# Attention values of layer 1 and of the stick-breaking block: attention weights as the stationary side, against values as the stationary side with two heads on the halves of the array's columns

## The chip, the core and the metric

The program runs on one core of one Trainium2 chip. The metric is device microseconds of one execution, the median of several runs. The program is one launch: weights are streamed from HBM, everything else stays on the core. The engines are TensorE (PE, with PEld for its weight loads), VectorE (DVE), ScalarE (ACT), GpSimd (POOL) and SyncE (SP), which issues the DMAs.

## What is computed

Two mixing layers and a second block, on 256 positions of width 1024, in float32. Two places matter here. Layer 1 (`moba_attention`) has 16 heads of 64; with 256 positions there is one block, so it is causal attention, followed by a gate and an output projection:

```python
s_own = jnp.einsum('bhqd,bhkd->bhqk', qc, kown).astype(jnp.float32)
p = masked_softmax(jnp.concatenate([s_sel, s_own], axis=-1) * scale, mask).astype(v.dtype)
o + jnp.einsum('bhqk,bhkd->bhqd', p[..., nk:], vown)
...
o = moba_attention(q, k, v, cos, sin) * jax.nn.silu(z)
return jnp.einsum('bse,ed->bsd', o, w_out)
```

The second block has a stick-breaking attention with 8 heads of 64, whose output goes into a projection without a gate of its own ahead of it:

```python
attn = jnp.where(causal, jnp.exp(jax.nn.log_sigmoid(z) + rest), 0.0)
return jnp.einsum("bhqk,bhkd->bhqd", attn.astype(v.dtype), v)
...
y_a = o @ w_attn_out[l]
```

## The kernel before

Positions lie in two tiles of 128 (`tt` = 0, 1). Each projection (`Proj`, line 694) accumulates a 128x512 output in an accumulator bank (`acc`), with three float32r matmuls for each 128 rows of the contraction (`mm3`, line 658): high by high, high by low and low by high part. Both sides are therefore split into a high part (ACT copy) and a low part (DVE subtraction): the weights after their DMA (`split`, line 651), the activations after a turn to feature-major on TensorE (`to_lhs`, line 827; the lists `oT`, `ya`, `hT` hold the two parts). These projections are the bulk of TensorE's work, the rows `acc<-kr,kr` of the profile.

In the names of the profile `k` stands for the plain SBUF pools, `kr` for the pool of split float32r tiles, `m` for the four working PSUM banks, `acc` for the four accumulators and `tiny` for small vectors. All instructions carry line 562 (or 563 in the changed kernel), that of the recording helper. Each float32 matmul of 128x64 and the like is two records in the trace, a transpose by the identity is one.

**Layer 1.** It works in two halves `j` of 8 heads. A unit (`o_unit`, line 1483, through `sm_unit`, line 883) takes four heads of tile 0 or two heads of tile 1: scores and a mask into one bank, maximum on DVE, exponential on ACT with the sum into `den1`, then a turn (four transposes, one ACT copy into `pt`), then the values: for each head and key block one matmul with the 128x128 piece of `pt` as the stationary side and the head's 64 columns of `v` as the moving side. There are 12 units, with four such matmuls each. The output is position-major, [128, 8, 64] in one bank for each (`j`, `tt`). `o_done` (line 1495) multiplies it by the reciprocal of twice the sums on DVE. `gated` (line 1344) multiplies by the gate `zz` (the silu of projection `odd3j`) on DVE and sends the product through `to_lhs`: four transposes, an ACT copy for the high part and a DVE subtraction for the low part. `mid1` (line 1531) does so for the second half of the heads, in the middle of the output projection `oo`.

**Stick-breaking.** `st_unit` (line 1703) makes one head: scores into a bank `z`, two ACT passes, a scan and a product on DVE, three transposes, one ACT copy `at`, then three value matmuls with 128x128 pieces of `at` stationary and 64 columns of `v` moving. After each four heads two ACT copies scale the bank into position-major tiles, and at the end `st_done` (line 1741) turns these with eight transposes, two ACT copies and two DVE subtractions into `ya`. Beside it DVE runs the 124 steps of a depthwise convolution (`conv_step`, line 1603), which are put in with a low priority.

**The order.** The program is recorded first, as a list of operations with their dependences. A list scheduler (`Order.solve`, line 284) then sets the order in which each engine's queue receives them, and the slots of the pools, from a table of durations (`cost`, line 508); `best` (line 271) takes the best of several rules and rounds. `od.fused()` ties consecutive operations into one that nothing is put between. Each engine runs its own queue in order and waits on semaphores. The order of one operation can therefore move others around it.

## Time and profile before

| | us |
|---|---|
| median of 3 runs | 759.78 |
| the three runs | 757.1, 759.78, 760.51 |
| the profiled execution, its own time | 761.01 |
| its span in the trace | 759.3 |
| TensorE busy | 733.1 (97%) |
| VectorE busy | 573.7 (76%) |
| ScalarE busy | 404.1 (53%) |
| granted TensorE clock, mean | 0.997 |

TensorE's busy time is the union of its records, whose ends are modelled; they overlap, so the mean of one record is longer than the time that it adds. The time of a matmul is better read from the starts of consecutive rows. Layer 1 attention lies between about 229 and 332 us of the span, the stick-breaking attention between about 390 and 468 us.

### The profile page before, as it was taken

What the parts mean: (1) busy time and instruction counts of PE and PEld (TensorE: products, weight loads), DVE (VectorE), ACT (ScalarE), POOL (GpSimd) and SP (SyncE); (2) the same over time, 40 slices, a digit from 0 to 9 for tenths busy, and PEclk for the clock granted to TensorE, in tenths of its full rate; (3) what the DMA queues carried; (4) which work ended last, traced back from release to release, by engine and by line L of the source; (5) the groups of instructions that cost most, each with busy time, mean ns of one, the idle gap of its engine ahead of it and who ended that gap; (6) DMA issues with size and microseconds to landing.
All of it is one profiled execution on the core that took longest, in us unless ns stands there. A gap on an engine that the chain in (4) does not pass through costs nothing.

```text
span 759.3 us, 10452 instructions
## 1 busy us (share of the span) xinstructions
PE 733.1 (97%) x3712; PEld 596.4 (79%) x3712; DVE 573.7 (76%) x1057; ACT 404.1 (53%) x715; POOL 13.7 (2%) x40
## 2 busy tenths in 40 slices
PE   3999999997999999999999999999999999999998
PEld 1887788786787888878877778878887888888886
DVE  4899899957987564598899999997857555646531
ACT  5565878747454546446455564566445444435420
POOL 1000000000000000001000000000000000000000
PEclk9999999999999999999999999999999999999999
DMA  8998978734684533456532476654747555645101
GB/s 325 400 372 285 368 251 297 236 130 140 210 289 136 196 129 114 148 191 209 182 113 84 139 226 208 206 184 174 250 139 253 191 195 173 214 140 193 57 1 55
DMA packets 43572, 148.08 MB, mean 195 GB/s; under 512 B 6272, under 2 KB 7424, under 8 KB 43520
## 3 DMA queue, kind: packets, MB, share of 16 engines
q1 hardware_dynamic: 43520, 147.41, 56.6%
q8 instruction: 29, 0.48, 0.3%
q14 instruction: 23, 0.19, 0.1%
HBM read 146.34 MB, written 1.05 MB: 194 GB/s over the span
## 4 chain that ended last, share of the span: by engine, by line
PE 76%; DVE 10%; DMA 7%; ACT 5%; issue 1%; SPq 0%; ACTq 0%; DVEq 0%
PE acc L562 65%; PE m L562 11%; DMA k<-in_wst_dram 7%; DVE k L562 5%; DVE kr L562 4%; ACT k L562 3%; ACT kr L562 2%; DVE x L562 1%; SPq L562 0%; DVE tiny L562 0%; DVE ab L562 0%; DVE keepA L562 0%; ACTq L562 0%; DVEq L562 0%
## 5 line engine op out<-in xcount | busy, mean ns | idle before, releaser
L562 PE MATMUL acc<-kr,kr 128*128 128x512 f32 x2520 | 653.7, 407 | 4.0 <-ACT kr L562 3.9
L562 PEld LDWEIGHTS acc<-kr,kr 128*128 128x128 f32 x2520 | 469.0, 190 | 103.2 <-ACT k L562 2.8
L562 DVE TENSOR_TENSOR kr<-k,kr 128x1024 fp32r<-128x1024 f32 (+3 forms) x234 | 265.9, 1151 | 85.8 <-PE acc L562 68.0
L562 ACT ACTIVATE kr<-k 128x1024 fp32r<-128x1024 f32 (+3 forms) x234 | 230.6, 1005 | 147.0 <-PE acc L562 98.1
L562 PE MATMUL m<-identf,k 128*128 128x128 f32 x414 | 97.5, 279 | 5.8 <-DVE k L562 4.8
L562 PE MATMUL m<-k,k 128*128 128x64 f32 (+4 forms) x436 | 75.3, 304 | 11.6 <-DMA k<-in_wst_dram 10.6
L562 PEld LDWEIGHTS m<-k,k 128*128 128x128 f32 (+1 forms) x436 | 67.1, 188 | 22.2 <-issue 12.2
L562 ACT ACTIVATE k<-m 128x512 f32<-128x512 f32 (+6 forms) x115 | 53.3, 471 | 39.7 <-PE m L562 38.3
L562 PEld LDWEIGHTS m<-identf,k 128*128 128x128 f32 x414 | 56.7, 146 | 20.8 <-DVE k L562 6.0
L562 DVE CUSTOM_DVE_ANT_0 k<-k,cb 128x1024 f32<-128x1024 f32 x44 | 53.0, 1216 | 2.4 <-DMA k<-in_wst_dram 2.3
L562 DVE SCALAR_TENSOR_TENSOR k<-k,col,k 128x256 f32<-128x256 f32 x128 | 54.2, 475 | 0.0
L562 ACT ACTIVATE k<-m,tiny 128x128 f32<-128x128 f32 (+1 forms) x80 | 32.9, 423 | 21.6 <-DVE tiny L562 18.9
L562 ACT ACTIVATE kr<-m 128x512 fp32r<-128x512 f32 (+3 forms) x52 | 24.9, 491 | 27.6 <-PE m L562 23.7
L562 DVE TENSOR_TENSOR kr<-m,kr 128x256 fp32r<-128x256 f32 (+2 forms) x44 | 23.8, 552 | 13.0 <-PE acc L562 7.5
L562 DVE TENSOR_REDUCE tiny<-m 128x2 f32<-128x512 f32 (+1 forms) x30 | 20.6, 687 | 7.8 <-PE m L562 7.5
L562 DVE TENSOR_TENSOR k<-k,k 128x512 f32<-128x512 f32 (+5 forms) x42 | 24.5, 591 | 0.3
L562 ACT ACTIVATE k<-acc,rf 128x256 f32<-128x256 f32 x22 | 10.3, 472 | 27.0 <-PE acc L562 26.8
L562 DVE SCALAR_TENSOR_TENSOR k<-acc,rf,k 128x256 f32<-128x256 f32 x22 | 10.5, 482 | 18.7 <-ACT k L562 18.5
L562 ACT ACTIVATE k<-k 128x512 f32<-128x512 f32 (+4 forms) x28 | 14.9, 538 | 13.6 <-DVE k L562 13.5
L562 PE MATMUL m<-kr,kr 128*128 128x408 f32 (+1 forms) x96 | 21.7, 329 | 0.1
L562 DVE TENSOR_TENSOR k<-acc,x 128x512 f32<-128x512 f32 x4 | 2.8, 691 | 22.4 <-PE acc L562 22.4
L562 ACT ACTIVATE k<-m,ab 128x128 f32<-128x128 f32 (+1 forms) x24 | 10.6, 489 | 14.9 <-DVE ab L562 14.9
(111 smaller groups left out, 319.9 us busy)
## 6 DMA issues: line engine op xcount, KB each, us to landing
k<-in_wst_dram SPq DMA_DIRECT2D x266, 512.0 KB, 4.5
k<-in_wst_dram SPq DMA_DIRECT2D x8, 204.0 KB, 8.1
k<-in_rows_dram SPq DMA_DIRECT2D x3, 512.0 KB, 3.5
k<-in_rows_dram SPq DMA_DIRECT2D x6, 256.0 KB, 5.5
x<-in_x_dram SPq DMA_DIRECT2D x2, 512.0 KB, 3.8
out_dram<-k SPq DMA_DIRECT2D x4, 256.0 KB, 2.0
cb<-in_rows_dram SPq DMA_DIRECT2D x1, 512.0 KB, 7.0
k<-in_w_dram SPq DMA_DIRECT2D x2, 128.0 KB, 5.9
```

The lines of the kernel that those rows point to most:

```text
L562: self._o.add(self._n, lambda: f(*a, **kw), method, writes, reads, info)
```

## The change

In layer 1 the roles of the value matmul are swapped: the 64 columns of `v` of one head are the stationary side, in one half of the array's columns, and the 128 columns of `pt` move. Two heads lie on the two halves (output partitions 0 to 63 and 64 to 127), and the four matmuls of a unit are tied together with `od.fused()`. Heads are now taken in sequence. The output is feature-major, [128, 4, 128]. The factor from the sums, which belongs to a position, can no longer be put on the output by a broadcast along its rows; it is put on the gate, position-major, and the gate is turned instead (`z_turn`): one DVE product, four transposes, one ACT copy. `o_done` copies the output out of PSUM with ACT; `gated_t` multiplies on DVE and splits into high and low part from SBUF.

In the stick-breaking block the values are swapped in the same way for a pair of heads at a time: two matmuls of 256 and two of 128 moving columns. The output is already feature-major, so the high and low parts are taken straight from PSUM, with the factor 0.5, and the two position-major tiles, the four scaling copies and `st_done` with its eight transposes are gone. The table of durations gets an entry for outputs of 64 partitions.

```diff
-            return (d / 4 + 20.0 if writes[0].ap[0][1] == 32 else d), 210.0, None
+            n = writes[0].ap[0][1]
+            return (d / 4 + 20.0 if n == 32 else d / 2 + 10.0 if n == 64 else d), 210.0, None
...
+            if give is not None:
+                return lambda: give(pt.rearrange("p (i b) q -> p i b q", b=kb))
...
     def o_unit(j, tt, u):
-        for i in range(n):
-            h = head(tt, u, i)
...
+        def values(pt):
+            o = get(o1, (j, tt), lambda: bank([P, 4, P], n="o1"))
+            with od.fused():
+                for i in range(0, n, 2):
+                    for b in range(tt + 1):
+                        for a in range(2):
+                            h = n * u + i + a
+                            PE.matmul(o[64 * a:64 * a + 64, h // 2, :], st["v", j][:, b, 64 * h:64 * h + 64], pt[:, i + a, b, :],
+                                      start=b == 0, stop=b == tt, skip_group_check=True)
...
     def o_done(j, tt):
-        o = t2([P, 8, 64], n="o")
-        V.tensor_tensor(o, o1[j, tt], cf[:, :, None].to_broadcast([P, 8, 64]), op=ALU.mult)
-        o1[j, tt] = o
+        o = t2([P, 4, P], n="o")
+        copy_act(o, o1[j, tt])
+        o1[j, tt] = o, cf
+
+    def z_turn(hf, tt, cf):
+        z = zz[hf][tt]
+        V.tensor_tensor(hv(z, 8), hv(z, 8), cf[:, :, None].to_broadcast([P, 8, 64]), op=ALU.mult)
+        p, g = bank([P, 4, P]), t2([P, 4, P], n="g")
+        for i in range(4):
+            PE.transpose(p[:, i, :], z[:, i * P:i * P + P], identf)
+        copy_act(g, p)
+        return g
+
+    def gated_t(o, g, tt, hf):
+        hi, lo = (a[hf][:, :, tt * P:tt * P + P] for a in oT)
+        V.tensor_tensor(o, o, g, op=ALU.mult)
+        copy_act(hi, o)
+        V.tensor_tensor(lo, o, hi.bitcast(F32), op=ALU.subtract)
...
     def st_unit(h):
+            ats[h] = at
+            if h % 2 == 0:
+                return lambda: None
             def values():
-                PE.matmul(o[:, 0, h % 4, :], at[:, 0:P], v[:, 0, :], start=True, stop=True, skip_group_check=True)
-                PE.matmul(o[:, 1, h % 4, :], at[:, P:256], v[:, 0, :], start=True, stop=False, skip_group_check=True)
-                PE.matmul(o[:, 1, h % 4, :], at[:, 256:384], v[:, 1, :], start=False, stop=True, skip_group_check=True)
+                o = get(os_, h // 4, lambda: bank([P, 2, 256], n="os"))[:, h // 2 % 2, :]
+                with od.fused():
+                    for b, (q0, q1, c) in enumerate(((0, 256, 0), (P, 256, 256))):
+                        for i in range(2):
+                            v = qk["v"][:, b, 64 * (h - 1 + i):64 * (h + i)]
+                            PE.matmul(o[64 * i:64 * i + 64, q0:q1], v, ats[h - 1 + i][:, c:c + q1 - q0], start=b == 0, stop=b == 1, skip_group_check=True)
                 if h % 4 == 3:
+                    b = h // 4
+                    hi, lo = (a[0][:, 2 * b:2 * b + 2, :] for a in ya)
+                    S.activation(hi, os_[b], AF.Copy, scale=0.5)
+                    V.scalar_tensor_tensor(lo, os_[b], 0.5, hi.bitcast(F32), op0=ALU.mult, op1=ALU.subtract)
...
-    def st_done():
-        for tt in range(2):
-            to_lhs(ya, os_["o"][tt].rearrange("p h d -> p (h d)"), tt, 0, 4)
```

The order of the queues stays the same up to the start of layer 1's attention, and again from the end of the stick-breaking block on; between them each queue is set anew.

TensorE's queue in layer 1, values of the second unit of the first half (`m_157` is the output bank; before, `k_107` is `pt` and `k_63` the values), in the kernel before:

```order
L562 LDWEIGHTS identb
L562 MATMUL m_156<-m_176,identb 128x2x128
L562 MATMUL acc_147<-kr_86,kr_100 128x512
L562 MATMUL m_157<-k_63,k_107 128x64
L562 MATMUL acc_147<-kr_97,kr_100 128x512
L562 MATMUL m_157<-k_63,k_107 128x64
L562 MATMUL acc_147<-kr_86,kr_79 128x512
L562 MATMUL m_157<-k_63,k_107 128x64
L562 MATMUL acc_150<-kr_80,kr_100 128x512
L562 MATMUL m_157<-k_63,k_107 128x64
```

The same place in the changed kernel (`k_113` is `pt`, `k_64` the values):

```order
L563 LDWEIGHTS identb
L563 MATMUL m_156<-m_176,identb 128x2x128
L563 MATMUL acc_148<-kr_86,kr_79 128x512
L563 MATMUL m_157<-k_113,k_64 64x128 x4
L563 MATMUL acc_150<-kr_80,kr_100 128x512
L563 MATMUL acc_148<-kr_80,kr_100 128x512
```

The four value matmuls stood one by one between projection matmuls; now they stand in one piece of four.

TensorE's queue in the stick-breaking block, values of one head in the kernel before (`m_155` is the output bank, `k_117` is `at`, `k_70` the values; the second head of the pair stands some 30 rows on, in the same form):

```order
L562 MATMUL acc_150<-kr_88,kr_92 128x512
L562 MATMUL m_155<-k_70,k_117 128x64
L562 MATMUL acc_149<-kr_102,kr_82 128x512
L562 MATMUL m_155<-k_70,k_117 128x64
L562 MATMUL acc_149<-kr_100,kr_98 128x512
L562 MATMUL m_155<-k_70,k_117 128x64
L562 MATMUL acc_150<-kr_100,kr_82 128x512
```

The values of the first pair of heads in the changed kernel (`m_157` is the output bank, `k_117` and `k_108` are the two `at`):

```order
L563 MATMUL acc_149<-kr_101,kr_97 128x512
L563 MATMUL m_157<-k_117,k_72 64x256
L563 MATMUL m_157<-k_108,k_72 64x256
L563 MATMUL m_157<-k_117,k_72 64x128
L563 MATMUL m_157<-k_108,k_72 64x128
L563 MATMUL acc_149<-kr_79,kr_81 128x512
```

Six matmuls of 64 moving columns for a pair became four of 256 or 128, in one piece.

TensorE's queue at the end of the stick-breaking block, the turn of the two finished tiles (`st_done`) in the kernel before:

```order
L562 MATMUL acc_147<-kr_97,kr_98 128x512
L562 MATMUL m_156<-identf,k_117 128x128
L562 MATMUL m_157<-identf,k_107 128x128
L562 MATMUL m_156<-identf,k_117 128x128
L562 MATMUL m_157<-identf,k_107 128x128
L562 MATMUL m_156<-identf,k_117 128x128
L562 MATMUL m_157<-identf,k_107 128x128
L562 MATMUL m_156<-identf,k_117 128x128
L562 MATMUL m_157<-identf,k_107 128x128
L562 MATMUL acc_148<-kr_97,kr_82 128x512
```

The same projection in the changed kernel:

```order
L563 MATMUL acc_149<-kr_92,kr_97 128x512
L563 MATMUL acc_148<-kr_84,kr_82 128x512
L563 MATMUL acc_149<-kr_93,kr_97 128x512
L563 MATMUL acc_148<-kr_103,kr_82 128x512
L563 MATMUL acc_149<-kr_92,kr_81 128x512
```

The eight transposes are gone, and the projection's matmuls follow one another.

## Rows read from the trace of the kernel before

**Rows 1.** The page: span, busy time of the engines, the ending chain by engine.
```profile
span 759.3 us, 10452 instructions
PE 733.1 (97%) x3712; PEld 596.4 (79%) x3712; DVE 573.7 (76%) x1057; ACT 404.1 (53%) x715; POOL 13.7 (2%) x40
...
PE 76%; DVE 10%; DMA 7%; ACT 5%; issue 1%; SPq 0%; ACTq 0%; DVEq 0%
```

**Rows 2.** Busy time by stretch; behind it TensorE's clock, DMA share and GB/s.
```profile
core 0: us, PE busy (x) PEld busy (x) DVE busy (x) ACT busy (x) POOL busy (x), PEclk, DMA share, GB/s
60.00:100.00 40.00, 39.00 (x277) 29.72 (x276) 37.79 (x92) 27.99 (x82) 0.99 (x3) 1.00 0.88 312
229.00:332.00 103.00, 101.40 (x556) 83.93 (x554) 63.67 (x90) 54.13 (x111) 1.89 (x2) 1.00 0.41 140
400.00:460.00 60.00, 58.35 (x302) 46.97 (x301) 59.94 (x115) 33.28 (x54) 0.26 (x2) 1.00 0.51 167
460.00:570.00 110.00, 110.00 (x508) 90.04 (x508) 93.43 (x149) 58.06 (x73) 0.00 (x0) 1.00 0.56 187
```

**Rows 3.** TensorE's waits from 230 to 575 us: total us, times, longest.
```profile
PE m L562 <- DVE k L562: 4.5, 7, 1.6
```

**Rows 4.** Timeline of TensorE in layer 1's values: start, us, instruction, count.
```profile
260.26 0.33 PE L562 MATMUL m<-k,k 128*128 128x64 f32 x2
260.40 0.48 PE L562 MATMUL acc<-kr,kr 128*128 128x512 f32 x1
260.72 0.33 PE L562 MATMUL m<-k,k 128*128 128x64 f32 x2
...
261.98 0.27 PE L562 MATMUL m<-identf,k 128*128 128x128 f32 x1
262.01 0.48 PE L562 MATMUL acc<-kr,kr 128*128 128x512 f32 x1
262.32 0.27 PE L562 MATMUL m<-identf,k 128*128 128x128 f32 x1
```

**Rows 5.** Timeline of TensorE in the stick-breaking block: values, a wait, a run, `st_done`.
```profile
399.50 0.33 PE L562 MATMUL m<-k,k 128*128 128x64 f32 x2
399.63 0.47 PE L562 MATMUL acc<-kr,kr 128*128 128x512 f32 x1
399.95 0.33 PE L562 MATMUL m<-k,k 128*128 128x64 f32 x2
...
412.75 0.30 PE L562 MATMUL m<-identf,k 128*128 128x128 f32 x1 [0.57 <-DVE k L562]
...
455.62 10.49 PE L562 MATMUL acc<-kr,kr 128*128 128x512 f32 x45
465.94 1.04 PE L562 MATMUL m<-identf,k 128*128 128x128 f32 x8
```

**Rows 6.** Timeline of TensorE where layer 0 uses quarters of the columns (128*32).
```profile
76.22 1.50 PE L562 MATMUL acc<-k,k 128*32 128x256 f32 x24
...
80.54 0.64 PE L562 MATMUL acc<-k,k 128*32 128x256 f32 x8
81.11 0.33 PE L562 MATMUL m<-identf,k 128*128 128x128 f32 x1
81.37 0.64 PE L562 MATMUL acc<-k,k 128*32 128x256 f32 x8
81.94 0.33 PE L562 MATMUL m<-identf,k 128*128 128x128 f32 x1
82.20 0.64 PE L562 MATMUL acc<-k,k 128*32 128x256 f32 x8
```

**Rows 7.** Groups by shape: count, busy us, mean ns of one, idle before it.
```profile
L562 PEld LDWEIGHTS m<-identf,k 128*128 128x128 f32 x414 | 56.7, 146 | 20.8 <-DVE k L562 6.0 <-ACT k L562 4.7 <-issue 4.2
L562 ACT ACTIVATE k<-m 128x512 f32<-128x512 f32 x41 | 24.5, 601 | 18.9 <-PE m L562 18.3
L562 DVE TENSOR_TENSOR k<-k,k 128x512 f32<-128x512 f32 x30 | 20.5, 686 | 0.3
```

More of the change, by code (lines that the diff above doesn't have):

```diff
@@ L881, in head, with sm_unit @@
         return 2 * i + u if tt == 0 else 4 * (u % 2) + 2 * i + u // 2
-    def sm_unit(tt, segs, klen, masks, o, den, sink=None):
+    def sm_unit(tt, segs, klen, masks, o, den, sink=None, give=None):
         ns = len(segs)
@@ L1484, in o_unit @@
         n = 4 if tt == 0 else 2
-        segs = []
-        for i in range(n):
-            h = head(tt, u, i)
-            segs.append(([(st["q", j][:, h // 2, tt * P:tt * P + P], st["k", j][h % 2][:, h // 2, 0:P * (tt + 1)])],
-                         [st["v", j][:, t, 64 * h:64 * h + 64] for t in range(tt + 1)], h))
+        segs = [([(st["q", j][:, h // 2, tt * P:tt * P + P], st["k", j][h % 2][:, h // 2, 0:P * (tt + 1)])], None, h)
+                for h in range(n * u, n * u + n)]
         kl = P * (tt + 1)
         masks = lambda s: (s[:, :, kl - P:kl], causal[:, None, :].to_broadcast([P, n, P]))
-        return sm_unit(tt, segs, kl, masks, lambda sl: get(o1, (j, tt), lambda: bank([P, 8, 64], n="o1"))[:, sl, :],
-                       lambda sl: den1[:, j, tt, sl:sl + 1])
+        def values(pt):
[7 more added lines that the diff above has]
+                                      start=b == 0, stop=b == tt, skip_group_check=True)
+        return sm_unit(tt, segs, kl, masks, None, lambda sl: den1[:, j, tt, sl:sl + 1], give=values)
     def o_done(j, tt):
@@ L1498, in o_done, with gated1 @@
         recip(cf, cf)
-        o = t2([P, 8, 64], n="o")
-        V.tensor_tensor(o, o1[j, tt], cf[:, :, None].to_broadcast([P, 8, 64]), op=ALU.mult)
-        o1[j, tt] = o
+        o = t2([P, 4, P], n="o")
[14 more added lines that the diff above has]
+        V.tensor_tensor(lo, o, hi.bitcast(F32), op=ALU.subtract)
+    def gated1(j, tt):
+        o, cf = o1[j, tt]
+        gated_t(o, z_turn(j, tt, cf), tt, j)
     def o_units(j):
@@ L1522, in program @@
     for tt in range(2):
-        after(1 + tt, lambda tt=tt: gated(o1[0, tt], tt, 0))
+        after(1 + tt, lambda tt=tt: gated1(0, tt))
     proj("odd31", hT, z_evict(1))
@@ L1533, in mid1 @@
         for tt in range(2):
-            gated(o1[1, tt], tt, 1)
+            gated1(1, tt)
         tk.drain()
@@ L1699, in v_evict @@
         scaled(get(qk, "v", lambda: t4([P, 2, 512], n="v"))[:, tt, :], acc, tt)
-    os_ = {}
+    os_, ats = {}, {}
+    ya = new_lhs(4)
     def st_unit(h):
@@ L1751, in program @@
     proj("p2", hT, v_evict)
-    every(2, 8, [launch(lambda h=h: st_unit(h)) for h in range(8)] + [lambda: None, lambda: None, st_done])
+    every(2, 8, [launch(lambda h=h: st_unit(h)) for h in range(8)])
     proj("p5", hT, sc_x)
```

6 lines of the change are left out of this document (removed).

## The prediction

> **What bounds the kernel now.** I read the page first: TensorE is busy for 97% of the span, and the chain that ends last lies on it for 76% [rows 1]. Then I cut the span into stretches. In layer 1's attention (229 to 332 us) TensorE is busy for 101.4 of 103 us, with ACT at 54.1 and DVE at 63.7. In the core of the stick-breaking block (400 to 460) it is busy for 58.35 of 60, and here DVE is full as well, 59.94 of 60. Behind it (460 to 570) TensorE is busy without a break, 110.0 of 110 [rows 2]. So what TensorE has less to do in these stretches ends the program earlier, unless it turns into a wait. The waits that there are: seven, 4.5 us in all, each a transpose that waits for a DVE result [rows 3]; one of them, 0.57 us, is seen in [rows 5]. The granted clock is 1.00 (the 2.4 GHz level) in all of these stretches, also in 60 to 100, where layer 0 runs matmuls on quarters of the columns [rows 2].
>
> **What one instruction costs on TensorE.** Records overlap, so I take starts. A projection matmul in a long run: 45 of them between 455.62 and 465.94, 10.32 / 45 = 0.229 us [rows 5]. A value matmul (two records) with a projection matmul behind it: 260.26 to 260.72, 0.46; so the value matmul adds 0.46 - 0.229 = 0.23 [rows 4]; in the stick-breaking block 399.50 to 399.95, 0.45, the same [rows 5]. I use 0.228. A transpose so embedded: 261.98 to 262.32 is 0.34, so it adds 0.11 [rows 4].
>
> Half columns are not in the trace, but quarters are. A piece of 8 records (four matmuls of 256 columns) takes 0.64, one of 24 takes 1.50 [rows 6]; 16 records more cost 0.86, so four records cost 0.215. A single record with 256 moving columns would by the same rate take as long by itself, so the four column groups run side by side. I take it that two halves do too: one wave of two records costs 0.215 for 256 moving columns and 0.1075 for 128.
>
> Going into the quarter mode and out of it has a price. Piece and transpose alternate from 80.54 to 81.37 to 82.20, a period of 0.83 [rows 6]; two waves are 0.43, the transpose 0.11; 0.29 is left for one way in and out. The Trainium skill says in TensorEngine Tiling (Array Packing), section Key Properties, that changing the tiling mode drains TensorE; the 0.29 us agree with that. The section Theoretical Speedup there gives up to 2x for a dimension of at most 64; by that alone, without the drain, the sum would be that of the first rival.
>
> In the changed kernel projection matmuls follow most pieces instead of transposes. Their weight load is longer (half of a value matmul's two loads, 0.114 at most, where the transpose's record is also shorter, 146 ns on the mean [rows 7]), and the piece's own first load has 64 columns instead of 32, at most 0.06 more. So the price of a piece lies between 0.29 and 0.29 + 0.11 + 0.06 = 0.46. I take 0.35, nearer to the end that was measured, since the transpose in between had a load of its own in the 0.29.
>
> **The change part by part.**
>
> Layer 1, values. Before, a unit has four value matmuls, 4 x 0.228 = 0.91. After, four half-column matmuls of 128 columns, two records each, are four waves: 4 x 0.1075 + 0.35 = 0.78. That saves 0.13 in each of 12 units: 1.6 us.
>
> Stick-breaking, values. Before, six matmuls for a pair of heads, 6 x 0.228 = 1.37. After, two waves of 256 and two of 128: 0.43 + 0.215 + 0.35 = 1.00. That saves 0.37 for each of four pairs: 1.5 us.
>
> Stick-breaking, the turn. Eight transposes go (the row at 465.94 [rows 5]), 8 x 0.11 = 0.9 us.
>
> Sum on TensorE: 4.0 us less. With the price of a piece at 0.29 it is 16 x 0.06 = 1.0 more, 5.0; with 0.46 it is 16 x 0.11 = 1.8 less, 2.2.
>
> What else moves, and its cover. The gate's turn has as many transposes as the output's turn had, four for each of four tiles: nothing on TensorE. On DVE each tile has three passes before (factor, gate, low part) and three after (factor on the gate, gate, low part), 0.69 each [rows 7]: nothing. On ACT each tile gets two passes more (the output out of PSUM, the turned gate), 0.60 each [rows 7]: 8 x 0.6 = 4.8 us in a stretch where ACT is idle for half of the time [rows 2], hidden by TensorE; the stick-breaking block loses four short ACT copies. No DMA is added or taken away. The chain from a finished gate to the split output is longer by an ACT copy and a DVE product, 0.60 + 0.69 = 1.3 us, and what waits for it are the projection matmuls of `oo` on the second half of the heads, and all that is queued behind them on TensorE. In the changed order some 19 projection matmuls (4.4 us) stand between the gate's transposes of the first tile and the first of these, and 36 between those of the second tile and theirs; the chain is two ACT passes and two DVE passes, 2.6 us and four hand-overs. So it is covered; bare, it would cost the 1.3 us, once. A fused piece waits as a whole for one ACT copy (`pt`, or the later of the two `at`), where single matmuls waited before for the same copy; the projection matmuls behind it would wait too.
>
> The order between 230 and 468 us is set anew, so the waits of [rows 3] in that stretch (that of 0.57 among them) come out differently. Nothing in the chain of a head from scores to transposes changes; I count zero, with 0.5 us to both sides.
>
> **Result.** The profiled execution took 761.01 us (span 759.3); less 4.0 is 757.0. It is the slowest of those known, 0.2% above the median of 759.78; on the median it gives 755.8. With the bounds of the price and of the waits its own range is 754.3 to 758.1.
>
> **Rivals.**
>
> 1. The way in and out costs nothing. A unit then saves 0.91 - 0.43 = 0.48 (12 times: 5.8), a pair 1.37 - 0.645 = 0.73 (four times: 2.9), the turn 0.9: 9.6 us, 750.2. Against it speaks the period of 0.83 [rows 6].
>
> 2. DVE takes the stick-breaking part back. DVE is full from 400 to 460 [rows 2] and transposes already wait for it [rows 5]. If each microsecond that TensorE gains there turns into such a wait, only layer 1's 1.6 us are left: 758.2. Against it: most of DVE's work there is the convolution, of low priority; after 460 TensorE never waits [rows 2].
>
> 3. The halves do not run side by side, and it gets slower. Quarters ran four at a time; with halves the two records of one matmul could go one after another with those of the other. A unit then costs 8 x 0.1075 + 0.35 = 1.21, 0.30 more than before (3.6 for 12 units), a pair 4 x 0.215 + 4 x 0.1075 + 0.35 = 1.64, 0.27 more (1.1), the turn still saves 0.9: 3.8 slower, 763.6. It decides once a wave of two records takes over about 0.14 us instead of 0.1075 in layer 1. The rows of the quarters [rows 6] speak against it.
>
> **Chances.** The forecast 0.67, rival 1 0.06, rival 2 0.17, rival 3 0.08, the rest something that I don't see. About 0.5% (3.8 us) is what a measurement of this kernel can tell from no change, and my 4.0 lies right on it: the forecast splits nearly evenly into faster and same. Faster by over 0.5%, below 756.0: half of the forecast with a little from its waits, and rival 1: 0.46. Slower by over 0.5%, above 763.6: half of rival 3 and a little: 0.05. The rest, 0.49, is within 0.5%. The range runs from 753.5, past the forecast's own lower end by what runs scatter (757.1 to 760.5 before), to 759.2, past rival 2 by 1.0; it leaves out rivals 1 and 3.
>
> **What would show it.** In the profile after: rows `m<-k,k` of 128*64 whose records start in twos within some 10 ns, with 0.11 (or 0.215) to the next two, each unit a row of x8, about 0.78 us from the projection matmul's place before it to normal running behind it. If the second of two records starts 0.1 us late, rival 3 holds. If pieces take 0.43 without more, rival 1. If TensorE's waits for DVE between 390 and 468 grow by 2 us, rival 2. The clock should stay at 1.00 there; ACT in layer 1's stretch should gain about 5 us; no waits should appear at the `oo` projection. The prediction is wrong if TensorE's busy time falls by 4 and the span does not, or if the pieces cost over 0.9.

## The result: 1.2% faster, twice the predicted gain

Four runs of the changed kernel took 749.18 to 751.26 us, median 750.47; four of the kernel before 757.1 to 760.51, median 759.67. The medians lie 9.2 us apart; the ratio is 0.9883, 95% interval 0.9855 to 0.991, that is between 6.8 and 11.0 us less. The forecast was 4.0 us less, 755.8, with a range from 753.5 to 759.2. The direction was right, the time lies 3 us below the range.

The profiled execution of the changed kernel took 750.70 us. The page, in the lines that answer to [rows 1]:

```profile
span 749.0 us, 10399 instructions
PE 725.4 (97%) x3688; PEld 582.9 (78%) x3688; DVE 573.0 (76%) x1057; ACT 405.8 (54%) x719; POOL 14.2 (2%) x40
...
PE 76%; DVE 12%; ACT 5%; DMA 5%; issue 2%; SPq 0%; DVEq 0%; ACTq 0%
```

TensorE is busy 7.7 us less (733.1 before) and the span is 10.3 us shorter. The same stretches as in [rows 2], moved by what the kernel is ahead at their place:

```profile
60.00:100.00 40.00, 39.26 (x279) 30.00 (x279) 38.09 (x92) 28.23 (x82) 0.99 (x3) 1.00 0.89 315
218.00:318.00 100.00, 99.91 (x559) 77.48 (x558) 65.52 (x95) 58.29 (x127) 1.90 (x2) 1.00 0.49 168
...
391.00:450.00 59.00, 58.09 (x295) 44.37 (x294) 58.89 (x109) 31.29 (x51) 0.25 (x2) 1.00 0.48 169
450.00:560.00 110.00, 109.82 (x504) 89.69 (x503) 95.32 (x159) 59.65 (x74) 0.00 (x0) 1.00 0.56 183
```

In layer 1 TensorE has next to no idle time left (0.09 of 100 us; 1.6 of 103 before), ACT has some 4 us more to do, and the granted clock stays at 1.00. DVE is as full in the stick-breaking block as before. TensorE's waits from 218 to 565 us, the stretch that answers to [rows 3]:

```profile
PE m L563 <- DVE k L563: 1.6, 4, 0.7
PE m L563 <- ACT k L563: 0.2, 1, 0.2
```

1.8 us instead of 4.5. The pieces themselves, in the timelines that answer to [rows 4] and [rows 5] (a unit of layer 1, then a pair of heads in the stick-breaking block):

```profile
259.14 1.64 PE L563 MATMUL acc<-kr,kr 128*128 128x512 f32 x6
260.71 0.66 PE L563 MATMUL m<-k,k 128*64 128x128 f32 x8
261.29 1.66 PE L563 MATMUL acc<-kr,kr 128*128 128x512 f32 x6
```

```profile
399.00 0.99 PE L563 MATMUL acc<-kr,kr 128*128 128x512 f32 x3
399.92 0.87 PE L563 MATMUL m<-k,k 128*64 128x256 f32 x8
400.72 0.96 PE L563 MATMUL acc<-kr,kr 128*128 128x512 f32 x3
```

From the single records: in this unit of layer 1 the eight start at 0, 0.007, 0.161, 0.167, 0.270, 0.277, 0.379 and 0.386 us, the next projection matmul at 0.588; in the pair of the other block they start at 0, 0.006, 0.267, 0.274, 0.483, 0.490, 0.592 and 0.599, the next at 0.801. Halves run side by side, and from one wave to the next it is 0.109 us (128 columns) or 0.216 (256). Going in, the first record of the pair starts 0.319 behind a projection matmul instead of 0.229; going out, the second projection matmul starts 0.338 behind the first (0.326 and 0.335 in the unit). A unit so costs 0.09 + 0.588 + 0.11 = 0.79 (predicted 0.78) and a pair 1.00 (predicted 1.00). **The pieces cost what was forecast; the other 5 us came from somewhere else.**

**Where they came from.** All kernels here have the same 2520 projection matmuls (`acc<-kr,kr`) in the same stages, so the start of the n-th serves as a milestone. Counting from 0, the 480th lies just ahead of layer 1's first values, the 1080th ahead of those of the stick-breaking block, the 1500th behind it; the 780th to 840th are the end of layer 1's output projection `oo`. Stage lengths in us, worked out from the starts in each kernel's profiled execution:

| kernel | layer 1, 480 to 1080 | 480-600 | 600-780 | 780-840 | stick, 1080 to 1500 |
|---|---|---|---|---|---|
| before | 180.67 | 43.42 | 61.41 | 16.97 | 116.73 |
| stick-breaking part alone | 181.04 | 43.75 | 61.40 | 17.00 | 113.92 |
| before, one DVE pass moved | 179.93 | 42.66 | 61.40 | 16.97 | 116.72 |
| before, two places moved | 181.36 | 43.09 | 61.51 | 17.83 | 116.66 |
| before, values tied | 180.54 | 43.20 | 61.50 | 16.95 | 116.62 |
| before, heads in sequence | 180.20 | 42.95 | 61.36 | 16.93 | 116.82 |
| layer 1's gate path alone | 179.02 | 41.89 | 61.31 | 16.93 | 116.59 |
| layer 1's values alone | 178.75 | 42.19 | 60.72 | 16.95 | 116.75 |
| layer 1's part | 176.03 | 41.38 | 60.69 | 15.50 | 117.66 |
| **changed** | 176.27 | 41.30 | 60.66 | 15.51 | 113.92 |
| changed, again | 176.19 | 41.20 | 60.68 | 15.51 | 113.92 |
| changed, old values in place | 177.71 | 41.86 | 61.54 | 15.51 | 114.88 |
| changed, pieces split | 180.25 | 42.63 | 63.29 | 15.51 | 114.87 |
| changed, all pieces joined | 175.53 | 41.56 | 59.69 | 15.49 | 114.40 |
| changed, half of them joined | 174.92 | 40.98 | 59.67 | 15.48 | 113.95 |
| changed, without the table's entry | 177.47 | 41.74 | 60.64 | 16.27 | 117.79 |

The stretch from 840 to 1080 takes 58.5 to 59.0 in all of them, and from the 1500th to the last of them it is 241.3 to 241.4. The stages repeat to 0.1 us where the order is the same (the two executions of the changed kernel), and to 0.4 where a DMA's landing enters. From the 480th on the changed kernel is 7.2 us ahead of the kernel before (7.6 ahead of the stick-breaking part's layer 1): **4.4 to 4.8 in layer 1, where 1.6 were forecast, and 2.8 in the stick-breaking block, where 2.4 were.** The rest of the 9.2 lies ahead of the 480th, where executions differ by up to 5 us (last section).

### The profile page after: what moved, and what is told of

It reads as the page before. It is cut to its first block, busy times and chain, and to the rows that moved or that the text cites. A ratio compares the mean times of both kernels' runs of the same rounds, so it can differ in the third digit from the quotient of the medians.

```text
span 749.0 us, 10399 instructions
## 1 busy us (share of the span) xinstructions
PE 725.4 (97%) x3688; PEld 582.9 (78%) x3688; DVE 573.0 (76%) x1057; ACT 405.8 (54%) x719; POOL 14.2 (2%) x40
## 4 chain that ended last, share of the span: by engine, by line
PE 76%; DVE 12%; ACT 5%; DMA 5%; issue 2%; SPq 0%; DVEq 0%; ACTq 0%
PE acc L563 66%; PE m L563 10%; DVE k L563 7%; DMA k<-in_wst_dram 5%; DVE kr L563 4%; ACT k L563 3%; ACT kr L563 2%; DVE tiny L563 1%; DVE x L563 0%; SPq L563 0%; DVE ab L563 0%; DVE keepA L563 0%; DVEq L563 0%; ACTq L563 0%
## 5 line engine op out<-in xcount | busy, mean ns | idle before, releaser
L563 PE MATMUL acc<-kr,kr 128*128 128x512 f32 x2520 | 641.1, 405 | 3.5 <-ACT kr L563 3.4
L563 DVE TENSOR_TENSOR kr<-k,kr 128x1024 fp32r<-128x1024 f32 (+3 forms) x238 | 268.9, 1144 | 80.5 <-PE acc L563 56.7
L563 PE MATMUL m<-k,k 128*128 128x64 f32 (+6 forms) x420 | 63.4, 321 | 11.5 <-DMA k<-in_wst_dram 10.7
L563 ACT ACTIVATE k<-m 128x512 f32<-128x512 f32 (+7 forms) x119 | 56.6, 481 | 32.7 <-PE m L563 31.4
L563 PEld LDWEIGHTS m<-k,k 128*128 128x128 f32 (+2 forms) x420 | 47.9, 171 | 24.2 <-issue 16.6
L563 ACT ACTIVATE kr<-m 128x256 fp32r<-128x256 f32 (+3 forms) x48 | 22.5, 481 | 11.5 <-PE m L563 11.4
L563 DVE TENSOR_TENSOR kr<-m,kr 128x256 fp32r<-128x256 f32 (+2 forms) x38 | 19.7, 531 | 7.3 <-ACT kr L563 3.6
L563 ACT ACTIVATE k<-acc,rf 128x256 f32<-128x256 f32 x22 | 10.3, 472 | 27.3 <-PE acc L563 27.1
L563 PEld LDWEIGHTS m<-kr,kr 128*128 128x128 f32 x96 | 15.9, 188 | 4.6 <-DVE kr L563 2.4
```

The lines of the kernel that those rows point to most:

```text
L563: self._o.add(self._n, lambda: f(*a, **kw), method, writes, reads, info)
```

## The experiments

Theory A: the value matmuls save what was forecast, and the rest is waits that the new order of the queues no longer has. Theory B: the swap itself saves more than forecast.

### Each part alone

Layer 1's part with the stick-breaking block of before, and the reverse.

> The change in layer 1 alone; stick-breaking as before. Up to the stick-breaking block every queue has the order of the changed kernel. Theory A (the value matmuls save what was forecast, 1.6 us here, and the rest of the gain is waits that the new order no longer has, 1.6 us at 232.8 and 0.5 us at 332 in the profile before, with what follows them): 759.7 - 1.6 - 2.1 = 756.0, or down to 754.9 if all that the two traces differ by between 216 and 397 us (4.9 us) is kept. Theory B (the pieces save more than forecast, in the same proportion everywhere: 9.2/4.0 of the forecast): 759.7 - 3.7 = 756.0. The time alone doesn't tell them apart; the trace does: under A no wait of TensorE for DVE over 0.2 us stands between 228 and 335 us and a piece still takes 0.78.

> The change in the stick-breaking block alone; up to there every queue has the order of the kernel before. Theory A: 2.4 us for values and transposes as forecast, and up to 0.9 us less waiting for DVE in the block: 759.7 - 2.4 to 3.3 = 756.4 to 757.3, with the waits of 1.6 us near 232.8 and 0.5 us near 332 still there. Theory B (all of the 9.2 us is value matmuls and transposes, in the forecast's proportion): 759.7 - 5.5 = 754.2.

Layer 1's part: 753.26 us, ratio 0.9934 (0.9915 to 0.9952), some 5.0 us less. Stick-breaking part: 755.28 us, ratio 0.9955 (0.9936 to 0.9975), some 3.4 less. The two add up to 8.4. The second is 756.3 on the 759.7 of the first comparison, at the low edge of what A expected, and its trace keeps layer 1's waits; B's 5.5 is out. The first is 754.7 on that scale, just below A's 754.9, and A's sign is there: no wait of TensorE for DVE is listed from 216 to 340 us, and the pieces are those of the changed kernel. All three stretches of layer 1 shrink, also 780-840, in which there is no value matmul at all: 16.97 to 15.50. Its stick-breaking block, with all instructions of before, is 0.9 us longer (117.66 instead of 116.73): a first case of an order that takes instead of giving.

### The old values in the new order

The order is planned with the pieces as they are; in the second pass over the program, which only issues, the matmuls of before stand in their place.

```diff
+            if found is not None:
+                with od.fused():
+                    for i in range(n):
+                        for b in range(tt + 1):
+                            h = n * u + i
+                            PE.matmul(o.rearrange("p c (a d) -> p (c a) d", a=2)[:, h, :], pt[:, i, b, :], st["v", j][:, b, 64 * h:64 * h + 64],
+                                      start=b == 0, stop=b == tt, skip_group_check=True)
+                return
```

The same for a pair in the stick-breaking block, with six matmuls.

> The changed kernel with its order of every queue unchanged, and in the place of each of the 16 pieces the matmuls of before (weights stationary, 64 columns of the values moving, 4 in a unit, 6 for a pair of heads, in one row); the outputs then lie where the next step doesn't expect them. Theory A: each piece costs more by what was forecast, 12 x 0.13 + 4 x 0.37 = 3.1 us: 753.5; the rest of the gain (5.2 us) stays, because it belongs to the order. Theory B: the gain of layer 1's and stick-breaking's values goes, 3.1/4.0 of 9.2 = 7.1 us: 757.6.

752.20 us, ratio 0.9918 (0.9897 to 0.9939), which is 753.5 on the 759.7 of the first comparison: A's number. The old matmuls stand in the places of the pieces:

```profile
257.93 0.85 PE L563 MATMUL acc<-kr,kr 128*128 128x512 f32 x3
258.62 1.00 PE L563 MATMUL m<-k,k 128*128 128x64 f32 x8
259.43 0.94 PE L563 MATMUL acc<-kr,kr 128*128 128x512 f32 x3
```

Against the changed kernel layer 1 is 1.4 to 1.5 us longer and the stick-breaking block 1.0. So of layer 1's 4.4 to 4.8 us the values are 1.5; **3.0 to 3.3 stay with the old values, and belong to the order and the gate path.** The table says where they lie. Against the kernel before, this run is 1.6 us shorter in 480-600, where the wait of 1.6 us near 232.8 stood, and 1.5 shorter in 780-840, where that of 0.53 near 332 stood; in 600-780, where no wait was, it is 0.1 longer. Of the other block's 2.8, 1.0 is values and 0.9 the eight transposes (by their starts in the kernel before); 0.9 is left for the waits there, of which the rows list 1.6 us before and 0.8 changed.

### The price of the column mode, in time

The pieces cut in two, with the order of all queues kept: the second half is issued behind the next TensorE instruction.

```diff
         for i in order:
             self.ops[i]()
+            if self.on[i] == "PE" and rest:
+                for call in rest:
+                    call()
+                rest = []
+            rest = rest + self.rest.get(i, [])
```

The reverse: the first piece of each two moved to just ahead of the second, for all 16 and then only where no wait came of it (`pieces[6:12:2]` with `pieces[7:12:2]`).

```diff
+        for i, j in zip(pieces[::2], pieces[1::2]):
...
+                order.remove(i)
+                order.insert(order.index(j), i)
```

> The changed kernel again, beside the three that differ from it in one point each, for more runs of both on one chip. Earlier: 9.2 us below the kernel before, interval 6.8 to 11. From the traces, counted from the 480th projection matmul on (from there the executions differ by the kernel only; ahead of it by up to 5 us among executions of the same order), the two kernels differ by 7.2 to 7.6 us: 0.9905 of the time before.

> The changed kernel with the order of every queue kept, but the second half of each of the 16 pieces put behind the next TensorE instruction, so that each piece becomes two. Theory A (one way into and out of the column mode costs 0.35 us, bounds 0.29 to 0.46): 16 x 0.35 = 5.6 us slower than the changed kernel (4.6 to 7.4). The rival, that the way is free and a piece costs its waves alone: no change.

> The changed kernel with the first piece of each two moved in TensorE's queue to just ahead of the second, so that 16 pieces become 8 rows of twice the length; nothing else moves in any queue. Theory A: 8 ways in and out less, 8 x 0.35 = 2.8 us faster than the changed kernel (2.3 to 3.7), unless what frees later (a bank, the tiles of the weights) makes something wait. The rival (the way is free): no change.

> The changed kernel with only the three pairs of pieces of layer 1's second half joined, where joining all of them brought no new wait (180 projection matmuls there took 59.69 instead of 60.66 us); the joins that made DVE waits in the first half and in the stick-breaking block are left out. Theory A: 1.0 us faster than the changed kernel, about 749; the rest of the order stays as it is, so nothing should give it back. The rival: the gain is lost to a wait before the end of layer 1, no change.

The changed kernel again: 749.54 us, 0.9877 (0.9854 to 0.9899), as in the first comparison and below the 0.9905 that the stages from the 480th on would give. Split: 755.68 us, 0.9951 (0.9934 to 0.9969), 6.1 us above it on the same chip, or 5.6 by the ratios; by the stages it is 5.0. Sixteen ways at 0.35 were 5.6. The rows show a half with what it costs:

```profile
256.85 0.44 PE L573 MATMUL m<-k,k 128*64 128x128 f32 x4
257.22 0.49 PE L573 MATMUL acc<-kr,kr 128*128 128x512 f32 x1
257.65 0.44 PE L573 MATMUL m<-k,k 128*64 128x128 f32 x4
258.01 0.96 PE L573 MATMUL acc<-kr,kr 128*128 128x512 f32 x3
```

Two waves of 0.109 occupy 0.37, and the projection matmul between the halves 0.43 instead of 0.229. Rival 1, the free way, is out.

All joined: 749.67 us, 0.9877 (0.9856 to 0.9899), no gain where 2.8 were expected. A joined row of 16 takes 1.02 (258.82 to 259.84), not twice 0.59, so the ways are saved; in 600-780 it shows, 59.69 instead of 60.66. Elsewhere it was given back: 480-600 and the stick-breaking block are 0.3 to 0.5 us longer than in the changed kernel. Waits of TensorE from 215 to 470 us in that run:

```profile
PE m L563 <- DVE k L563: 2.6, 4, 1.2
PE m L563 <- ACT k L563: 0.4, 1, 0.4
```

With only the second half of layer 1 joined layer 1's stage is shorter by 1.3 (176.2 to 174.9), of which 1.0, the expected gain, lies in 600-780 where the joins are, and no wait of TensorE is listed from 218 to 385 us; the time, 749.43 us, 0.9876 (0.9857 to 0.9896), can't tell 1 us. So this version is not shown to beat the changed kernel.

A further kernel tied only the two heads of one wave and let the scheduler plan anew:

> The changed kernel with the ties cut: only the two heads of one wave are tied, so 15 of the 16 pieces fall into two with other matmuls between. If one way into and out of the column mode costs 0.35 us (bounds 0.29 to 0.46), 15 x 0.35 = 5.3 us more than the changed kernel: 755.7 (754.8 to 757.4). If the way costs nothing, 750.5. The order of all queues is planned anew from the start, which by itself may move the time by some 2 us to either side.

757.77 us, 0.9985 (0.9968 to 1.0003). It tells nothing of the price by its time: the new plan differs from layer 0 on, and its 480th projection matmul starts at 217.1, against 212.0 to 213.5 in the two executions of the changed kernel. From the 480th to the 1500th it takes 3.8 us more than the changed kernel (294.0 against 290.2), less than the 15 ways at their lowest bound (4.4), so the new plan moved other things there as well. That is why the order was kept in the runs above.

### Which part of layer 1's change brings the other 3 us

Both parts of layer 1 apart, in the kernel before: the gate path alone (with the value matmuls of before), and the values alone (with the gate path of before).

> The kernel before with only the second part of layer 1's change: output copied out by ACT, factor on the gate, gate turned, product and split from SBUF; the value matmuls are those of before, untied, so their outputs don't lie as the next step takes them. Stick-breaking as before. Layer 1 (480th to 1080th projection matmul) took 180.7 to 181.0 us before and 176.0 to 176.3 changed, of which the values are 1.5 (the run with the old values in the new order). Theory A1 (the other 3.0 us are luck of the order): anything from 178 to 182 here. Theory A2 (they belong to the gate path: DVE has fewer passes where it is late, and the chain behind the output ends earlier): 178 or less, with no wait near 232 and none at the end of the output projection.

> The kernel before with only the first part of layer 1's change: the pieces, tied, heads in sequence, and the new entry of the table; the way from the output through factor, gate and turn is that of before, so it takes the outputs other than they lie. The end of the output projection has the order of before (alternating accumulators), so 60 projection matmuls there should again take 16.9 to 17.0 us with a wait of 0.53. Theory A: layer 1 is shorter by the values' 1.5 us and by what the order does near 232 (0 to 1.8): 177.4 to 179.5. If the values' part brought all of layer 1's gain: 176.2.

Gate path alone: 757.19 us, 0.9975 (0.996 to 0.9989). Values alone: 754.24 us, 0.9944 (0.9928 to 0.996). By stages the first gains 1.7 us, 1.5 of it in 480-600. The second gains 1.9: 0.7 in 600-780, where half of the pieces are, and 1.2 in 480-600. Neither touches 780-840. So layer 1 takes 179.0 with the gate path alone: that is in A1's range and not A2's 178 or less, though the wait near 232 is nearly gone. With the values alone it takes 178.75, as A expected. In 480-600 the two gain 2.8 together where both at once gain 2.1, since the wait there can go only once; 780-840 shrinks only with both. TensorE's waits from 216 to 240 us, of the kernel before, of the gate path alone and of the values alone (the changed kernel lists none there):

```profile
PE m L562 <- DVE k L562: 1.6, 1, 1.6
```

```profile
PE m L563 <- DVE k L563: 0.2, 1, 0.2
```

```profile
PE m L563 <- DVE k L563: 1.1, 1, 1.1
```

So the wait at 232.8 comes out otherwise in every plan. These kernels also differ in their instructions, and how much of it the gate path takes away by itself isn't separated from the order. What the wait is made of stands in the waits of all engines from 224 to 238 us, of the kernel before:

```profile
ACT kr L562 <- DMA k<-in_wst_dram: 2.2, 2, 1.1
DVE k L562 <- DMA k<-in_wst_dram: 2.0, 2, 1.1
...
PE m L562 <- DVE k L562: 1.6, 1, 1.6
```

Passes that take freshly loaded weights stand in DVE's and ACT's queues ahead of the passes that TensorE needs, and wait for their DMA. At the same place of the changed kernel (220 to 234 us there, since it is 3 to 5 us ahead) no wait of ACT or DVE for a DMA is listed; ACT waits 2.8 us for one just ahead of it, until 217.6, and no wait of TensorE is listed from 210 to 224 us.

### The same instructions in another order

Four kernels change nothing but the order. One moves a single DVE pass of the kernel before (the pass for the next layer's gate rows, and the DMA into its slot) behind the rotary sums; two change what the scheduler is told of layer 1 (a tie around the four value matmuls; the heads in sequence); one takes the new entry out of the table of durations.

```diff
+        late = [2054, 2151]
+        for i in late:
+            order.remove(i)
+        at = order.index(1687) + 1
+        order[at:at] = late
```

```diff
+                with od.fused() if tie else ExitStack():
+                    for i, (_, vs, sl) in enumerate(segs):
...
-            h = head(tt, u, i)
+            h = n * u + i
...
-            return (d / 4 + 20.0 if n == 32 else d / 2 + 10.0 if n == 64 else d), 210.0, None
+            return (d / 4 + 20.0 if n == 32 else d), 210.0, None
```

> The kernel before with one DVE pass moved in DVE's queue: the pass of the next layer's gate rows that waited 1.07 us for its weights' DMA at 231.5 us now stands behind the rotary sums (and the DMA that reuses its slot behind it); TensorE's, ACT's and SP's queues keep their order. Theory A (the transposes at 232.8 wait for the rotary sum, which stands behind that pass; order, not value matmuls): the wait of 1.6 us falls under 0.3 us and the time by 1.3 to 1.9 us. Theory C (TensorE would have to wait there anyway, for the accumulators or for another DVE pass): the wait comes back within the next 5 us, no change in the time.

> The kernel before with nothing changed but a tie around the four value matmuls of each unit in layer 1, so that the scheduler lays the queues of layer 1 out anew (before 200 us and behind layer 1 they are the same). Theory A (3.8 us of layer 1's 5.4 us in the traces come from the order, which any new plan may find or lose): the time moves by up to 3.8 us although no instruction is saved, down to 755; the waits at 232.8 and 332 change or go. Theory B (the swap of the sides brings it): within 1 us of the kernel before.

> The kernel before with the heads of layer 1 taken in sequence, as in the changed kernel, and nothing else: the same instructions, only layer 1's order planned anew. Theory A: the time moves by up to 3.8 us to either side with the waits at 232.8 and 332. Theory B: within 1 us of the kernel before.

> The changed kernel without the new entry in the table of durations: the same instructions, another order from the middle of layer 1 to the end of the stick-breaking block. Theory A: the values' part stays, the waits come out otherwise: 750.5 with up to 3 us to either side, and the difference is found in waits for DVE or ACT. Theory B (the gain is in the value matmuls): 750.5 within 1 us.

**The moved pass:** 757.08 us, 0.9986 (0.9968 to 1.0005). The wait of 1.6 us became one of 0.7 us, and its releaser changed; the lines of the same stretch:

```profile
ACT kr L562 <- DMA k<-in_wst_dram: 3.0, 3, 1.8
...
PE m L562 <- ACT k L562: 0.7, 1, 0.7
```

DVE no longer waits for a DMA. Now an ACT pass that splits freshly loaded weights does, and the copy that TensorE needs is queued behind it. So 0.8 to 1.1 us of the stage are gained, not 1.6, and neither theory had it: as the two traces read, the wait is not one pass in the wrong place, but weights that land late while several passes stand in line for them.

**Tied, and heads in sequence:** 757.09 us, 0.9982 (0.9966 to 0.9998) and 757.02 us, 0.9989 (0.9973 to 1.0005). Layer 1 is 0.1 to 0.8 us shorter; the waits at 232 and at 332 are still there (0.9 and 0.5; 1.1 and 0.5). A new plan alone does move the stage, but these two found little: some 1.1 us by the medians, which lies in theory A's range and next to B's 1 us and doesn't tell them apart.

**Without the table's entry:** 754.68 us, 0.9956 (0.9941 to 0.9971) against 0.9877 to 0.9883. No instruction of the program differs from the changed kernel. In the profiled execution it loses 1.2 us in layer 1 and 3.9 us in the stick-breaking block, where its waits from 385 to 470 us are:

```profile
PE m L563 <- ACT k L563: 1.6, 1, 1.6
PE m L563 <- DVE k L563: 1.3, 3, 0.9
```

A part of the 3.9 is clock. Behind the wait for ACT, which ends at 429.26, the granted clock fell to its lower level of 1.2 GHz (0.50 from 431 to 434); in no other kernel of the table does it fall below 1.00 between 200 and 480 us. The stretch:

```profile
428.00:436.00 8.00, 6.64 (x32) 4.51 (x33) 7.48 (x17) 4.30 (x8) 0.00 (x0) 0.79 0.18 72
```

A clock of 0.79 on the mean over 8 us is some 1.7 us lost (an estimate, 0.21 x 8.00), so 3.4 of the 5.1 us are order by itself. Two executions of this kernel had a clock of 1.00 on the mean, 752.32 and 754.0 us; that is 3.7 more than the changed kernel's five such (749.45 on the mean).

So one number in the planner's table, which changes no instruction, is worth nearly the whole forecast gain: more than the 3 us that theory A allowed, and theory B's 1 us is out. That all of layer 1's 3.0 us are order is not shown by it: this plan gives back 1.2 of them.

### The wait at the end of the output projection

In the kernel before (the row with the wait is one of the seven of [rows 3]), then in the changed kernel, TensorE's timeline:

```profile
330.01 0.60 PE L562 MATMUL m<-identf,k 128*128 128x128 f32 x4
330.36 1.86 PE L562 MATMUL acc<-kr,kr 128*128 128x512 f32 x7
332.76 1.25 PE L562 MATMUL m<-identf,k 128*128 128x128 f32 x8 [0.53 <-DVE k L562]
```

```profile
324.75 0.48 PE L563 MATMUL acc<-kr,kr 128*128 128x512 f32 x1
325.07 0.27 PE L563 MATMUL m<-identf,k 128*128 128x128 f32 x1
325.09 3.25 PE L563 MATMUL acc<-kr,kr 128*128 128x512 f32 x13
328.18 0.49 PE L563 MATMUL m<-identf,k 128*128 128x128 f32 x3
```

Before, the last two accumulators alternate and end together; DVE then has six passes to make for both, and TensorE has seven projection matmuls left to do meanwhile. In the changed kernel the accumulators end one after the other, with thirteen in between. All kernels with the first pattern show 16.9 to 17.0 us in 780-840 (16.27 in the one without the table's entry), all with the second 15.5. I tried to make the second pattern by hand in the kernel before, with the moved DVE pass as well (the numbers are those of recorded operations; `put` takes a list out and sets it behind the operation named):

```diff
+        put([2054, 2151], 1687)
+        put([2338, 2339, 2340, 2355, 2356, 2357], 2337)
+        put([2341, 2342], 2340)
```

> The kernel before, all instructions as they are, with two places of the order changed by hand: (1) as in the run with the moved DVE pass; (2) at the end of layer 1's output projection the last matmuls of its two accumulators no longer alternate (one accumulator's three first, then the other's six), and DVE does the three passes of the first ahead of those of the second. Layer 1 (480th to 1080th projection matmul) took 180.7 to 181.0 us; (1) alone gave 179.9. Theory A (the 3 us of layer 1 that the values don't explain are two waits that the order makes, near 232.8 and near 332, where 60 projection matmuls take 16.97 us before and 15.51 after): (2) takes 0.8 to 1.3 us more away, 178.6 to 179.1, on the time 1.8 to 2.3 us less than before. The rival (TensorE has to wait there for something that the order doesn't set): 179.9 stays.

758.36 us, 1.0001 (0.9984 to 1.0019): it got worse, 17.83 us in 780-840. The rows say why:

```profile
328.48 0.60 PE L562 MATMUL m<-identf,k 128*128 128x128 f32 x4
330.65 0.66 PE L562 MATMUL m<-identf,k 128*128 128x128 f32 x4 [1.57 <-DVE k L562]
```

The first four transposes no longer wait, but I had left a split of weights (1.22 us on DVE) between the two chains, and counted from the 780th projection matmul the second chain ended 0.9 us later than before. So that this wait depends on the order of the queues is shown, in the wrong direction; that the kernel before could reach 15.5 by order alone is not.

## Why the prediction was wrong, step by step

| step | predicted | measured |
|---|---|---|
| halves side by side, a wave of 128 / 256 columns | 0.1075 / 0.215 | 0.109 / 0.216 |
| one way into and out of the mode | 0.35 (0.29 to 0.46) | 0.35 in the rows, 0.31 to 0.38 by the split run |
| a unit of layer 1 / a pair of heads | 0.78 / 1.00 | 0.79 / 1.00 |
| layer 1's values | 1.6 | 1.5 (stage, old values in place) |
| stick-breaking values | 1.5 | 1.0 in the stage |
| eight transposes | 0.9 | 0.88 by their starts before; no run takes them apart |
| waits between 230 and 468 us | 0, with 0.5 to both sides | what the stages have left: 3.0 in layer 1, 0.9 in the stick-breaking block |

**The step that failed** is the last: "the order between 230 and 468 us is set anew, so the waits of [rows 3] in that stretch come out differently ... I count zero, with 0.5 us to both sides". The bound had no ground. [rows 3] listed 4.5 us of waits, and I looked at one of them, that of 0.57. The longest, 1.6 at 232.8, lay in layer 1's own stretch. All but the last, 0.73 near 571 us (which the change left as it is), could go, 3.8 us, and a new order could as well have made new ones. A bound from those rows would have been some 4 us to each side, and the range 750 to 761 instead of 753.5 to 759.2, with the measured 750.5 just inside its edge. The reason that I gave, that nothing in the chain of a head changes, was true and beside the point: the longest wait was made by other passes in the same queues, which waited for weights, and that at 332 by six DVE passes for two accumulators at once. What the stages have left in layer 1 lies where these two stood. Whether the gate path helped to remove them, beside the order, stays open. The price of 0.35, by contrast, was right, but it was a choice within 0.29 to 0.46; that it fits to 0.01 is in part luck.

**A wait is longer than its row.** [rows 3] counts idle time from the modelled end of the matmul ahead. At 332 the projection matmul ahead starts at 331.83 and the first transpose at 332.76, 0.93 later where 0.23 is normal: 0.70 of waiting where the row says 0.53. The eight transposes then take 1.34 instead of 0.88, since the second four wait again without a row of their own. So the row's 0.53 is at least 1.16, of the 1.46 that the stretch loses.

**The stick-breaking values** saved 0.34 for each pair on TensorE's rows, as forecast (six old matmuls in a row take 1.25 and cost 1.34 with their neighbours, the piece 1.00), but with the old values put back the stage grew by 1.0, not by 1.4. The run with the old values also has fewer waits there (0.5 us listed instead of 0.8), and DVE is full (58.89 of 59 us), so what TensorE saves is in part waited for. That is the mechanism of rival 2, with less than a third of what the values save there. One argument against that rival was too strong: behind 460 TensorE has no idle time up to 570, but the last wait of [rows 3], 0.73, stands at 571.

**Rival 1** gave 750.2, next to the measured 750.5, and is wrong all the same: a unit's piece would cost 0.43 by it and costs 0.79, and cutting the pieces in two cost about what sixteen ways cost. A time that fits doesn't prove its mechanism. The Trainium skill says in TensorEngine Tiling (Array Packing), section Key Properties, that changing the tiling mode drains TensorE; the 0.35 us here agree. **Rival 3** is out: the two records of a wave start 7 ns apart.

The covers held: no wait of TensorE is listed from 322 to 390 us, so the longer chain from the gate to the split output cost nothing, and neither did ACT's 4 us more.

## What to carry to other kernels

When a change makes a list scheduler lay out a stretch anew, the waits that stand in that stretch, read from starts and not from their rows alone, say about how much the order can give, and it can take as much: here the rows listed 3.8 us, the change found 3.9 beyond its own savings, and one number of the table lost 3.4 of it again. Ask of each long wait what is queued ahead of the pass that ends it. To price an edit apart from the order, keep the order and change only what is issued in its place, and compare stages by milestones that all versions share: here they repeat to 0.1 to 0.4 us, where the interval of a ratio spans 2 to 4 us. A mode that costs 0.35 us to enter and leave wants long pieces, but a piece that is held back for its partner is given back as a wait wherever another engine is full.

## What else the runs showed of the hardware

The price of the column mode has three parts, from the starts of single records: 0.09 ahead of the first record, 0.15 within the piece (0.160 from the first wave to the second and 0.21 from the last to the next projection matmul, instead of 0.109), 0.11 for the projection matmul behind it. Between transposes it is somewhat less: the first record behind a transpose starts 0.09 later than it would, but a transpose behind a piece adds only 0.06 (the projection matmul behind it starts 0.085 later, where 0.027 is usual).

Ahead of the 480th projection matmul executions of one order differ by up to 5 us. Much of it is one place: near 172 and 185 us TensorE waits up to 2.6 us for ACT's split of freshly loaded weights, and in some executions the granted clock then falls to the 1.2 GHz level for a part of what follows. Twelve microseconds from there, in the kernel before and in the changed one (the clock is the figure behind POOL's):

```profile
184.00:190.00 6.00, 3.89 (x15) 2.82 (x14) 3.46 (x6) 3.65 (x9) 0.00 (x0) 0.86 0.00 0
190.00:196.00 6.00, 6.00 (x26) 4.79 (x25) 4.85 (x5) 1.66 (x2) 0.95 (x1) 0.86 0.25 77
```

```profile
184.00:190.00 6.00, 4.33 (x19) 3.28 (x18) 4.88 (x7) 3.71 (x7) 0.53 (x1) 1.00 0.00 0
190.00:196.00 6.00, 6.00 (x29) 4.75 (x28) 6.00 (x8) 1.66 (x2) 0.42 (x1) 1.00 0.49 176
```

In the first, seventeen projection matmuls behind the wait take 5.56 us from start to start (187.73 to 193.29), 1.7 more than at 0.229. It fell behind the second of these waits in four of the eight profiled executions with layer 1's plan of before or a part of its change, and in one of the eight with the changed plan. In two more of each group it fell behind the first wait, and the second wait then was gone. The 480th projection matmul starts at 212.7 to 216.5 in the former group and at 210.8 to 213.9 in the latter, 1.9 us apart in the mean. That is what is missing between the 7.2 us of the stages and the 9.2 us of the medians.

How much of it belongs to the change? Up to the 388th projection matmul, at 188 to 193 us, TensorE's order is the same in all these traces, and that of the other engines up to about the same time; there, some 35 us ahead of layer 1's attention, the plans part. From the 400th to the 480th the kernel before takes 20.2 us and the changed one 19.8, so 0.4 more belongs to the order, and from the place where the plans part the two are 7.7 to 8.0 us apart. The rest goes with the clock. Of the executions whose clock is on record, 20 of 97 of the kernel before and 5 of 10 of the changed one had a granted clock of 1.00 on the mean; among these alone the means are 757.25 and 749.45 us, 7.8 apart. And a plan is not seen to spare the clock: it was 1.00 in 44 of 181 executions with layer 1's plan of before or a part of its change, and in 14 of 50 with the changed plan. So of the 9.2 us some 1.4 look like chance; five executions are too few to settle it.
